# A hybrid attention block: the memory's norm, keys and values move behind the first half's output projection

## The chip, the cores and the metric

The kernel runs on one core of one Trainium2 chip. Its time is the device time of one execution in microseconds (us); the kernel before takes 900.56 us, the median of three runs (899.28 to 900.87). An execution is also recorded by the hardware profiler; the numbers of the trace come from that one. The engines are TensorE (PE: matmuls; PEld: its weight loads), VectorE (DVE), ScalarE (ACT), GpSimd (POOL) and SyncE (SP), which only issues DMAs here. L96 is line 96 of the kernel before.

## The reference

One transformer block on x of 512 rows by 1024, with a memory of 256 rows by 1024. What matters here is its middle part (`_rmsnorm` scales each row by its root mean square and a gain):

```python
# inside the mixer: three branches o_a, o_b, o_c of width 256, gated and summed
g = sigmoid(p['g_merge']).reshape(B, S, 3, D_MODEL)
merged = g[..., 0, :] * (o_a @ w_up[0]) + g[..., 1, :] * (o_b @ w_up[1]) + g[..., 2, :] * (o_c @ w_up[2])
h = x + merged @ w_out                                   # the output projection

def _memory_attention(h, mem, g_q, g_kv, w_q, w_kv, w_o):
    q = (_rmsnorm(h, g_q) @ w_q).reshape(B, S, 4, 64)
    kv = (_rmsnorm(mem, g_kv) @ w_kv).reshape(B, M, 2, 4, 64)
    s = einsum('bshd,bmhd->bhsm', q, kv[:, :, 0]) * 64 ** -0.5
    o = einsum('bhsm,bmhd->bshd', softmax(s), kv[:, :, 1])
    return o.reshape(B, S, 256) @ w_o

h = h + _memory_attention(h, mem, ...)
h = h + _swiglu(_rmsnorm(h, norm_ffn), ...)              # the feed-forward stage (FFN)
```

The keys and values `kv` depend on the memory alone, so they can be computed at any point ahead of the first attention that reads them.

## The kernel before, in words

Every product of fp32 matrices is three matmuls of rounded halves: `mm3` (L91 to L96) issues high by high (L94), high by low (L95) and low by high (L96). An operand's halves are made by `split`: the high one is a cast on ScalarE (L58), the low one a subtraction (L66) on VectorE or GpSimd. A weight tile of 128 by 1024 is fetched by SP (L80) into `raw`, cast into `whi`, subtracted into `wlo`. There are two loaders: `load_split` with three buffers and the subtraction on VectorE, and `load_fill` with two buffers and the subtraction on GpSimd.

The order of the instructions on each engine is not written by hand: a scheduler takes the program and orders it by its own estimates, pools and dependencies. Each engine then runs its list strictly in that order, and an instruction that waits holds up all behind it.

The stretch that the change concerns, in the order of the program before:

1. Gates 2 and `merge_up(2, "c")`: gates of the third branch (`merge_gate`, tanh at L373), then its up projection, whose product is added to the running sum `g_t[0, f]` by GpSimd (L404), for eight feature blocks f.
2. Gates 1, first half: `fill_gate(1, f, S // 2)` for f = 0 to 7, 24 matmuls of 256 columns each into one of two banks `gf`; only the first 256 rows of x.
3. The memory stage (L661 to L683). Two memory chunks of 128 rows are loaded by ScalarE's queue into `h[0]` and `h[1]` (L664), normalised by `norm_t` (L122 to L137: a square with its sum on ScalarE, L127; eight small operations on VectorE, L115 to L120, for the root; the scaling, L129; eight transposes on TensorE, L133; high and low halves into `mem_t`, which is the second half of `mg`), multiplied by `w_mem_kv` in 48 matmuls of 512 columns into the two banks `gm` (L675), copied out; the keys are transposed (L680) into `km` and the values copied into `vm`.
4. `merge_up(1, "b")` for the first half: 48 matmuls of 256 columns, L388 and L401 on VectorE, the halves of the merged rows into the first half of `mg`. Then eight copies (L688, ScalarE) of the second half of the sums into `h[2]` and `h[3]` (`first1`).
5. The loop over halves (L778 on), cp = 0: x into `h[0]`, `h[1]` (L783); the output projection `ob`, 96 matmuls of 512 columns with eight tiles of `w_out` (L790); four adds into h (L794); `memory_pair` (L718): the norm with `gain_q`, the query projection, scores, softmax, the product with the values, the output matrix `w_mem_o`, the adds (L773), and the norm with `gain_f` for the FFN.
6. cp = 1 begins with `merge_rest` (L700): the gates and up projection of the first branch-1 features for the second half. Their matmuls (of 256 columns, into banks `wo`) need nothing of the first half's attention, and the scheduler sets them between the attention's steps, where TensorE would else wait. Then the same as in 5 for the second half, then the FFN.

The names of the tiles: `ut_hi`, `ut_lo` the halves of a normalised and transposed input; `u` the normalised rows; `ss`, `rs` the sum of squares and its root; `prm` the attention's probabilities; `gh` a gate of the second half.

## Time and profile before

| what | value |
|---|---|
| median of 3 runs | 900.56 us (899.28 to 900.87) |
| the profiled execution | 898.28 us |
| its span in the trace | 896.5 us, clock 0.994 of full |
| TensorE busy | 856.3 us (96%), 5012 matmuls and transposes |
| VectorE, ScalarE, GpSimd busy | 507.8, 411.5, 140.7 us |
| the stretch 374.7 to 476.0 us (points 3 to 6) | 101.3 us, TensorE busy 94.9 us |

A row of the trace has the start of an instruction (or of a run of equal ones, then xN), its duration, its engine and line, what it writes and reads, and in brackets how long the engine stood idle before it and which instruction released it. Matmuls overlap, so the time that one costs in a run is the distance between two starts and not its own duration. A window's row gives busy times in a stretch; its length less TensorE's busy time is the idle time there.

### The profile page before, as it was taken

Reading aid. Unit: us, or ns where it says so; the run is one execution under the profiler, and the core shown is the slowest. Engines: PE = TensorE matmul, PEld = TensorE weight load, DVE = VectorE, ACT = ScalarE, POOL = GpSimd, SP = SyncE. Lnnn points to the kernel's source line nnn. Section 1 sums busy time; section 2 is a strip of 40 time slices with the busy share of each in tenths; the row PEclk is TensorE's granted clock in tenths of the full one; section 3 lists DMA queues with packets and bytes.
Section 4 is the critical chain, followed back from the end, with each engine's and each line's share of the span. In section 5 each row is a group of like instructions: output and inputs, shape, how many; then the busy total and the mean of one; then the engine's idle time right before and its main releaser. Section 6 shows DMA issues by size and latency. Waiting matters only on the chain.

```text
span 896.5 us, 13084 instructions
## 1 busy us (share of the span) xinstructions
PE 856.3 (96%) x5012; PEld 731.7 (82%) x5012; DVE 507.8 (57%) x1155; ACT 411.5 (46%) x779; POOL 140.7 (16%) x116
## 2 busy tenths in 40 slices
PE   5999999899989999999989999999999999999995
PEld 5987899787757788978878979988888888888884
DVE  4456378799998305676677758643443334322226
ACT  6487545557774224544654545432322333211123
POOL 4021232302211347430232010000000000000002
PEclk9999999999999999999999999999999999999998
DMA  9340124510210334558446514642333332333312
GB/s 323 85 110 24 43 58 119 141 48 24 70 26 24 95 94 141 187 174 246 125 150 199 165 49 142 187 142 94 97 102 105 97 94 94 118 94 95 99 42 94
DMA packets 93710, 99.00 MB, mean 110 GB/s; under 512 B 4656, under 2 KB 81616, under 8 KB 93648
## 3 DMA queue, kind: packets, MB, share of 16 engines
q1 hardware_dynamic: 91568, 92.75, 34.0%
q10 hardware_dynamic: 2080, 5.42, 1.9%
q8 instruction: 39, 0.64, 0.3%
q14 instruction: 23, 0.19, 0.1%
HBM read 96.06 MB, written 2.10 MB: 109 GB/s over the span
## 4 chain that ended last, share of the span: by engine, by line
PE 85%; DVE 7%; ACT 4%; issue 2%; DMA 1%; POOL 0%; ACTq 0%; DVEq 0%; POOLq 0%
PE wo L95 9%; PE wo L96 9%; PE wo L94 9%; PE gf L94 6%; PE gf L95 6%; PE gf L96 6%; PE ff L94 4%; PE ff L95 4%; PE ff L96 4%; PE gm L94 3%; PE gm L95 3%; PE gm L96 3%; PE y L96 2%; PE y L94 2%; PE y L95 2%; PE av L101 2%
## 5 line engine op out<-in xcount | busy, mean ns | idle before, releaser
L58 ACT CAST whi<-raw 128x1024 fp32r<-128x1024 f32 (+1 forms) x167 | 174.8, 1048 | 292.4 <-PE y L96 78.9
L66 DVE TENSOR_TENSOR wlo<-raw,whi 128x1024 fp32r<-128x1024 f32 (+1 forms) x131 | 164.1, 1255 | 211.2 <-ACT whi L58 210.9
L66 POOL TENSOR_TENSOR wlo<-raw,whi 128x1024 fp32r<-128x1024 f32 x36 | 88.9, 2474 | 312.9 <-ACT whi L58 267.1
L95 PE MATMUL wo<-ut_lo,whi 128*128 128x256 f32 (+1 forms) x320 | 105.2, 329 | 0.0
L96 PE MATMUL wo<-ut_hi,wlo 128*128 128x256 f32 (+1 forms) x320 | 104.6, 327 | 0.0
L94 PE MATMUL wo<-ut_hi,whi 128*128 128x256 f32 (+1 forms) x320 | 104.4, 326 | 0.0
L96 PE MATMUL gf<-ut_hi,wlo 128*128 128x512 f32 (+1 forms) x192 | 69.8, 363 | 0.0
L94 PE MATMUL gf<-ut_hi,whi 128*128 128x512 f32 (+1 forms) x192 | 69.3, 361 | 0.0
L95 PE MATMUL gf<-ut_lo,whi 128*128 128x512 f32 (+1 forms) x192 | 69.3, 361 | 0.0
L94 PE MATMUL ff<-ut_hi,whi 128*128 128x512 f32 (+1 forms) x192 | 67.9, 354 | 0.0
L95 PE MATMUL ff<-ut_lo,whi 128*128 128x512 f32 (+1 forms) x192 | 67.9, 354 | 0.0
L96 PE MATMUL ff<-ut_hi,wlo 128*128 128x512 f32 (+1 forms) x192 | 67.9, 354 | 0.0
L95 PEld LDWEIGHTS wo<-ut_lo,whi 128*128 128x128 f32 x320 | 60.9, 190 | 6.2 <-issue 1.0
L94 PEld LDWEIGHTS wo<-ut_hi,whi 128*128 128x128 f32 x320 | 60.8, 190 | 5.8 <-issue 0.7
L96 PEld LDWEIGHTS wo<-ut_hi,wlo 128*128 128x128 f32 x320 | 60.8, 190 | 5.6 <-issue 0.4
L875 POOL TENSOR_TENSOR ut_hi<-ut_hi,ut_lo 128x512 f32<-128x512 f32 x4 | 5.0, 1276 | 367.0 <-ACT ut_hi L874 367.0
L94 PE MATMUL gm<-whi,ut_hi 128*128 128x256 f32 (+1 forms) x160 | 47.4, 296 | 0.0
L95 PE MATMUL gm<-wlo,ut_hi 128*128 128x256 f32 (+1 forms) x160 | 46.4, 290 | 0.0
L96 PE MATMUL gm<-whi,ut_lo 128*128 128x256 f32 (+1 forms) x160 | 46.3, 289 | 0.0
L96 PEld LDWEIGHTS gf<-ut_hi,wlo 128*128 128x128 f32 x192 | 36.2, 188 | 5.6 <-issue 1.2
L95 PEld LDWEIGHTS gf<-ut_lo,whi 128*128 128x128 f32 x192 | 36.2, 188 | 5.4 <-issue 0.8
L94 PEld LDWEIGHTS gf<-ut_hi,whi 128*128 128x128 f32 x192 | 36.2, 188 | 5.3 <-issue 0.8
(329 smaller groups left out, 2027.7 us busy)
## 6 DMA issues: line engine op xcount, KB each, us to landing
raw<-in_w_ffn_in_dram SPq DMA_DIRECT2D x56, 512.0 KB, 3.6
raw<-in_w_in_dram SPq DMA_DIRECT2D x46, 512.0 KB, 3.9
raw<-in_w_ffn_out_dram SPq DMA_DIRECT2D x22, 512.0 KB, 3.5
raw<-in_w_out_dram SPq DMA_DIRECT2D x16, 512.0 KB, 3.6
raw<-in_w_up_dram SPq DMA_DIRECT2D x8, 512.0 KB, 4.0
xt<-in_x_dram SPq DMA_DIRECT2D x4, 512.0 KB, 9.0
raw<-in_w_mem_kv_dram SPq DMA_DIRECT2D x4, 512.0 KB, 3.8
raw<-in_w_mem_q_dram SPq DMA_DIRECT2D x4, 512.0 KB, 3.8
```

Of the source, the lines that this page charges most:

```text
L58: nc.scalar.copy(dst, src)
L66: (lo_eng or nc.vector).tensor_sub(dst_lo, src, dst_hi.bitcast(F32))
L94: nc.tensor.matmul(dst, lh, rh, start=first, stop=False, skip_group_check=True)
L95: nc.tensor.matmul(dst, lh, rl, start=False, stop=False, skip_group_check=True)
L96: return nc.tensor.matmul(dst, ll, rh, start=False, stop=last, skip_group_check=True).ins
L101: nc.tensor.matmul(dst[64 * x:64 * x + 64], lhs[x], rhs[x], start=first, stop=last, skip_group_check=True)
L875: nc.gpsimd.tensor_mul(yo[:, n], yo[:, n], gain[:, n])
```

## The change

The memory stage goes from its place ahead of `merge_up(1, "b")` into a function `memory_kv()`, called after the first half's output projection is issued and before its adds into h. The raw memory rows then lie in the attention's `prm` tiles and no longer in `h[0]`, `h[1]`; the normalised rows in the pool's `u`; the keys in `qs`; the accumulators are the attention's two banks `mm` in place of `gm`; the transposes use the later pool of banks, which has two. `gain_kv` and `gain_q` take the two gain buffers, and `gain_f` is loaded after `memory_kv()` and handed to `memory_pair`. `mem_t` is still the second half of `mg`.

```diff
--- before.py
+++ after.py
@@ -658,30 +658,6 @@
     mg = (mgp.tile([P, NK, S], F32R, name="mg_hi"), mgp.tile([P, NK, S], F32R, name="mg_lo"))
     half0, half1 = slice(0, S // 2), slice(S // 2, S)
     mem_t = [t[:, :, half1] for t in mg]
-    kv_st = ctx.enter_context(ExitStack())
-    kvp = pool(kv_st, "kvp")
-    for c in range(2):
-        nc.scalar.dma_start(h[c], A["mem"][0, cc(c), :])
-    gain = load_gain(kvp, "norm_mem_kv")
-    for c in range(2):
-        norm_t(kvp, ps, h[c], gain, mem_t, cc(c), u=h[2 + c])
-    kv_acc = [gm_ps.tile([P, 512], F32, name="gm") for c in range(2)]
-    for k2 in range(0, NK, 2):
-        wh, wl = load_split((2, 512), [col_view(A["w_mem_kv"][0], 0, 512)[:, k2:k2 + 2, :]])
-        for kk in range(2):
-            for c in range(2):
-                k = k2 + kk
-                mm3(kv_acc[c], [t[:, k, cc(c)] for t in mem_t], (wh[:, kk, :], wl[:, kk, :]), k == 0, k == NK - 1)
-    for c in range(2):
-        kvt = h[c][:, 0:512]
-        nc.scalar.copy(kvt, kv_acc[c])
-        tp = ps.tile([P, 4, P], F32, name="ps")
-        for i in range(2):
-            nc.tensor.transpose(tp[:, i, :], kvt[:, i * P:(i + 1) * P], ident)
-        nc.vector.tensor_copy(km[:, :, cc(c)], tp[:, 0:2, :])
-        nc.vector.tensor_copy(vm[:, c, :], kvt[:, 256:512])
-    kv_st.close()
-
     merge_up(1, "b", load_split, gm_ps, S // 2)
     first1 = [h[2 + f // 4][:, f % 4 * 256:f % 4 * 256 + 256] for f in range(NK)]
     for f in range(NK):
@@ -712,10 +688,31 @@
             nc.vector.tensor_add(t, t, first1[f])
             split(mg[0][:, f, half1], mg[1][:, f, half1], t, lo_eng=nc.gpsimd)
 
+    gain_kv = load_gain(md, "norm_mem_kv", 2)
     gain_q = load_gain(md, "norm_mem_q", 2)
-    gain_f = load_gain(md, "norm_ffn", 2)
-
-    def memory_pair(cs):
+
+    def memory_kv():
+        for c in range(2):
+            raw = md.tile([P, 4, 256], F32, name="prm", bufs=2).rearrange("p a b -> p (a b)")
+            nc.scalar.dma_start(raw, A["mem"][0, cc(c), :])
+            norm_t(md, ps, raw, gain_kv, mem_t, cc(c))
+        acc = [mm_ps.tile([P, 512], F32, name="mm") for c in range(2)]
+        for k2 in range(0, NK, 2):
+            wh, wl = load_split((2, 512), [col_view(A["w_mem_kv"][0], 0, 512)[:, k2:k2 + 2, :]])
+            for kk in range(2):
+                for c in range(2):
+                    k = k2 + kk
+                    mm3(acc[c], [t[:, k, cc(c)] for t in mem_t], (wh[:, kk, :], wl[:, kk, :]), k == 0, k == NK - 1)
+        for c in range(2):
+            kt = md.tile([P, 256], F32, name="qs")
+            nc.scalar.copy(kt, acc[c][:, 0:256])
+            nc.vector.tensor_copy(vm[:, c, :], acc[c][:, 256:512])
+            tp = ps.tile([P, 4, P], F32, name="ps")
+            for i in range(2):
+                nc.tensor.transpose(tp[:, i, :], kt[:, i * P:(i + 1) * P], ident)
+            nc.vector.tensor_copy(km[:, :, cc(c)], tp[:, 0:2, :])
+
+    def memory_pair(cs, gain_f):
         pr = {}
         for c in cs:
             norm_t(md, ps, h[c], gain_q, uT, cc(c))
@@ -788,11 +785,14 @@
                 for half in range(2):
                     n = slice(half * 512, half * 512 + 512)
                     mm3(ob[c, half], [t[:, k, cc(c)] for t in mg], [t[:, 0, n] for t in w], k == 0, k == NK - 1)
+        if cp == 0:
+            memory_kv()
+            gain_f = load_gain(md, "norm_ffn", 2)
         for c in cs:
             for half in range(2):
                 n = slice(half * 512, half * 512 + 512)
                 nc.vector.tensor_add(h[c][:, n], ob[c, half], h[c][:, n])
-        memory_pair(cs)
+        memory_pair(cs, gain_f)
     dump("h2", h[0])
     mg_st.close()
```

The number of instructions is the same on every engine (1057 rows on VectorE in both lists). On the page of lines, L680 to L683 become L709 to L713, L688 becomes L664, L712 becomes L688, L773 becomes L770; the others named here keep theirs. Since `h[2]`, `h[3]` are no longer used by the memory's norm, the eight copies of `first1` move ahead into gates 1. The scheduler's order moves with it, on VectorE above all, at three places.

VectorE at the up projection of the first half, before (`g_4143`, `g_4176`, ... are the gates f = 0, 1, ...; `wlo_4710` is the first tile of `w_out`):

```order
L388 SCALAR_TENSOR_TENSOR g_4143<-g_4143,gm_4578 128x256
L401 TENSOR_TENSOR g_1119<-g_1119,g_4143 128x256
L388 SCALAR_TENSOR_TENSOR g_4176<-g_4176,gm_4589 128x256
L388 SCALAR_TENSOR_TENSOR g_4209<-g_4209,gm_4600 128x256
L401 TENSOR_TENSOR g_1152<-g_1152,g_4176 128x256
L401 TENSOR_TENSOR g_1185<-g_1185,g_4209 128x256
L388 SCALAR_TENSOR_TENSOR g_4242<-g_4242,gm_4611 128x256
L388 SCALAR_TENSOR_TENSOR g_4275<-g_4275,gm_4628 128x256
L401 TENSOR_TENSOR g_3551<-g_3551,g_4242 128x256
L401 TENSOR_TENSOR g_3584<-g_3584,g_4275 128x256
L388 SCALAR_TENSOR_TENSOR g_4308<-g_4308,gm_4639 128x256
L66 TENSOR_TENSOR wlo_4710<-raw_4707,whi_4709 128x1024
```

and after the change (`wlo_4429`, `wlo_4479` are the tiles of `w_up`, `wlo_4564` and `wlo_4582` the first two of `w_out`):

```order
L66 TENSOR_TENSOR wlo_4429<-raw_4426,whi_4428 128x1024
L66 TENSOR_TENSOR wlo_4479<-raw_4476,whi_4478 128x1024
L388 SCALAR_TENSOR_TENSOR g_4143<-g_4143,gm_4432 128x256
L66 TENSOR_TENSOR wlo_4564<-raw_4561,whi_4563 128x1024
L401 TENSOR_TENSOR g_1119<-g_1119,g_4143 128x256
L388 SCALAR_TENSOR_TENSOR g_4176<-g_4176,gm_4443 128x256
L388 SCALAR_TENSOR_TENSOR g_4209<-g_4209,gm_4454 128x256
L401 TENSOR_TENSOR g_1152<-g_1152,g_4176 128x256
L401 TENSOR_TENSOR g_1185<-g_1185,g_4209 128x256
L388 SCALAR_TENSOR_TENSOR g_4242<-g_4242,gm_4465 128x256
L401 TENSOR_TENSOR g_3551<-g_3551,g_4242 128x256
L388 SCALAR_TENSOR_TENSOR g_4275<-g_4275,gm_4482 128x256
```

The first tile of `w_out` is split ahead of the first gate's sum, where it stood behind that of the sixth.

VectorE at the norm of the second memory chunk, before (`gain_4431` is the memory's gain; the three `wlo` are tiles of `w_mem_kv`):

```order
L129 SCALAR_TENSOR_TENSOR h3_4415<-h1_4413,rs_4461,gain_4431 128x1024
L66 TENSOR_TENSOR wlo_4490<-raw_4487,whi_4489 128x1024
L66 TENSOR_TENSOR wlo_4508<-raw_4505,whi_4507 128x1024
L66 TENSOR_TENSOR wlo_4526<-raw_4523,whi_4525 128x1024
L66 TENSOR_TENSOR mg_lo_4425<-ps_4445,mg_hi_4424 128x4x128
L66 TENSOR_TENSOR mg_lo_4425<-ps_4452,mg_hi_4424 128x4x128
L66 TENSOR_TENSOR mg_lo_4425<-ps_4471,mg_hi_4424 128x4x128
L66 TENSOR_TENSOR mg_lo_4425<-ps_4478,mg_hi_4424 128x4x128
```

and after (`u_4737` is the second normalised chunk, `wlo_4786` and `wlo_4804` are tiles of `w_mem_kv`, `wo_4558` is the output projection's second sum for `h[0]`; the add of the first sum stands two rows further up):

```order
L66 TENSOR_TENSOR wlo_4786<-raw_4783,whi_4785 128x1024
L120 SCALAR_TENSOR_TENSOR rs_4739<-rs_4739 128x1
L794 TENSOR_TENSOR h0_4412<-wo_4558,h0_4412 128x512
L129 SCALAR_TENSOR_TENSOR u_4737<-prm_4734,rs_4739,gain_4551 128x1024
L66 TENSOR_TENSOR mg_lo_4425<-ps_4720,mg_hi_4424 128x4x128
L66 TENSOR_TENSOR mg_lo_4425<-ps_4727,mg_hi_4424 128x4x128
L66 TENSOR_TENSOR wlo_4804<-raw_4801,whi_4803 128x1024
L66 TENSOR_TENSOR mg_lo_4425<-ps_4749,mg_hi_4424 128x4x128
```

The scaling of the second chunk now stands behind the adds into `h[0]`, which need sums of the output projection, and the low halves of both chunks behind that.

VectorE at the norm for the FFN, before (`rs_5115` and `u_5113` belong to chunk 0):

```order
L119 SCALAR_TENSOR_TENSOR rs_5115<-rs_5115 128x1
L120 SCALAR_TENSOR_TENSOR rs_5115<-rs_5115 128x1
L129 SCALAR_TENSOR_TENSOR u_5113<-h0_4412,rs_5115,gain_4699 128x1024
L115 TENSOR_SCALAR rs_5142<-ss_5139 128x1
L117 TENSOR_SCALAR rs_5142<-rs_5142 128x1
L119 SCALAR_TENSOR_TENSOR rs_5142<-rs_5142 128x1
L66 TENSOR_TENSOR wlo_5483<-raw_5480,whi_5482 128x1024
```

and after (`gh_5168` to `gh_5234` are gates of the second half, `wo_5306` and so on their up projections, `rs_5117` and `u_5115` those of chunk 0):

```order
L119 SCALAR_TENSOR_TENSOR rs_5117<-rs_5117 128x1
L388 SCALAR_TENSOR_TENSOR gh_5168<-gh_5168,wo_5306 128x256
L120 SCALAR_TENSOR_TENSOR rs_5117<-rs_5117 128x1
L688 TENSOR_TENSOR gh_5168<-gh_5168,h2_4414 128x256
L119 SCALAR_TENSOR_TENSOR rs_5117<-rs_5117 128x1
L388 SCALAR_TENSOR_TENSOR gh_5201<-gh_5201,wo_5317 128x256
L120 SCALAR_TENSOR_TENSOR rs_5117<-rs_5117 128x1
L115 TENSOR_SCALAR rs_5144<-ss_5141 128x1
L688 TENSOR_TENSOR gh_5201<-gh_5201,h2_4414 128x256
L129 SCALAR_TENSOR_TENSOR u_5115<-h0_4412,rs_5117,gain_4851 128x1024
L117 TENSOR_SCALAR rs_5144<-rs_5144 128x1
L388 SCALAR_TENSOR_TENSOR gh_5234<-gh_5234,wo_5328 128x256
```

Sums of the gates for the second half, which stood in the softmax before, stand between the steps of the root; behind them, past the halves of chunk 0, comes the split of the next gate's weights.

## Rows read from the trace of the kernel before

**Rows 1.** Which engine sets the end: the page's busy time, share and count of each engine.

```profile
PE 856.3 (96%) x5012; PEld 731.7 (82%) x5012; DVE 507.8 (57%) x1155; ACT 411.5 (46%) x779; POOL 140.7 (16%) x116
```

**Rows 2.** The span in stages: busy time and count by engine, clock, DMA share, GB/s.

```profile
374.70:389.00 14.30, 13.59 (x67) 10.70 (x66) 7.57 (x9) 9.66 (x19) 0.81 (x1) 1.00 0.53 171
389.00:396.40 7.40, 7.06 (x54) 6.42 (x54) 6.73 (x16) 4.04 (x8) 3.86 (x5) 1.00 0.66 215
396.40:420.15 23.75, 22.34 (x97) 17.60 (x96) 15.68 (x17) 9.64 (x12) 5.03 (x4) 1.00 0.77 236
420.15:435.80 15.65, 15.38 (x131) 15.20 (x130) 11.84 (x28) 9.34 (x15) 1.44 (x1) 1.00 0.53 146
435.80:461.00 25.20, 23.81 (x164) 19.44 (x163) 17.38 (x32) 15.77 (x36) 8.86 (x7) 1.00 0.47 148
461.00:476.00 15.00, 12.76 (x106) 12.35 (x105) 14.26 (x28) 8.73 (x15) 3.28 (x2) 1.00 0.47 144
```

**Rows 3.** TensorE where the memory stage stands now: start, length, operation, idle before and releaser.

```profile
374.73 1.47 PE L133 MATMUL ps<-cst,h 128*128 128x128 f32 x12
...
376.67 0.50 PE L94 MATMUL gm<-whi,mg_hi 128*128 128x512 f32 x1 [0.47 <-ACT mg_hi L58]
...
377.65 0.51 PE L94 MATMUL gm<-whi,mg_hi 128*128 128x512 f32 x1 [0.25 <-ACT mg_hi L58]
...
378.35 0.48 PE L96 MATMUL gm<-whi,mg_lo 128*128 128x512 f32 x1
```

**Rows 4.** TensorE in the output projection of the first half, and its end.

```profile
400.81 0.50 PE L95 MATMUL wo<-wlo,mg_hi 128*128 128x512 f32 x1 [0.65 <-DVE wlo L66]
...
409.37 0.50 PE L95 MATMUL wo<-wlo,mg_hi 128*128 128x512 f32 x1 [0.77 <-DVE wlo L66]
...
419.93 0.39 PE L96 MATMUL wo<-whi,mg_lo 128*128 128x512 f32 x1
420.15 0.28 PE L94 MATMUL wo<-ut_hi,whi 128*128 128x256 f32 x1
420.26 0.28 PE L95 MATMUL wo<-ut_lo,whi 128*128 128x256 f32 x1
```

**Rows 5.** ScalarE: the gates' tanh, the load of a gain, and a weight cast that waits for DMA.

```profile
354.89 0.39 ACT L373 ACTIVATE g<-gf 128x256 f32<-128x256 f32 x1 [0.85 <-PE gf L96]
...
399.66 0.34 ACTq L140 DMA_DIRECT2D gain<-in_norm_mem_q_dram  x1
...
407.00 1.05 ACT L58 CAST whi<-raw 128x1024 fp32r<-128x1024 f32 x1 [5.35 <-DMA raw<-in_w_out_dram]
```

**Rows 6.** GpSimd: adds of the third branch, and a weight split beside the norm.

```profile
346.07 10.77 POOL L404 TENSOR_TENSOR g<-g 128x512 f32<-128x512 f32 x7
...
462.79 2.39 POOL L66 TENSOR_TENSOR wlo<-raw,whi 128x1024 fp32r<-128x1024 f32 x1 [0.90 <-POOL wlo L66]
```

**Rows 7.** VectorE: prices of an add into h and of a weight split.

```profile
418.31 0.69 DVE L794 TENSOR_TENSOR h<-wo,h 128x512 f32<-128x512 f32 x1 [0.71 <-PE wo L96]
418.92 1.22 DVE L66 TENSOR_TENSOR wlo<-raw,whi 128x1024 fp32r<-128x1024 f32 x1
```

**Rows 8.** TensorE at the transposes for the query projection.

```profile
426.45 1.06 PE L133 MATMUL ps<-cst,u 128*128 128x128 f32 x8 [0.27 <-DVE rs L120]
```

**Rows 9.** VectorE in the norm for the feed-forward stage of the first half.

```profile
462.90 2.30 DVE L120 SCALAR_TENSOR_TENSOR rs<-rs 128x1 f32<-128x1 f32 x1
...
465.68 1.28 DVE L129 SCALAR_TENSOR_TENSOR u<-h,rs,gain 128x1024 f32<-128x1024 f32 x1
...
468.52 1.28 DVE L66 TENSOR_TENSOR ut_lo<-ps,ut_hi 128x512 fp32r<-128x512 f32 x2
...
475.80 0.41 DVE L712 TENSOR_TENSOR gh<-gh,h 128x256 f32<-128x256 f32 x1
```

**Rows 10.** TensorE in the same norm: the last gate matmul, the transposes that wait.

```profile
464.50 0.28 PE L94 MATMUL wo<-ut_hi,whi 128*128 128x256 f32 x1
467.02 1.09 PE L133 MATMUL ps<-cst,u 128*128 128x128 f32 x8 [2.24 <-DVE u L129]
```

## The prediction

> **What bounds the kernel now.** I read the page's busy times first: TensorE is busy for 856.3 of 896.5 us, no other engine for more than 57% [rows 1]. The same matmuls are issued before and after the change, so it can only move TensorE's idle time. Next I read the windows by stage: from 374.7 to 476.0 us they show the granted clock at 1.00, which is the 2.4 GHz level, in every stage, and TensorE busy for 13.59 of 14.30, 7.06 of 7.40, 22.34 of 23.75, 15.38 of 15.65, 23.81 of 25.20 and 12.76 of 15.00 us, 94.9 of 101.3 in all [rows 2]. Then the timelines, for what ends each idle time. In the output projection it is twice the split of a weight tile on VectorE (0.65 and 0.77 us) [rows 4]; at the memory stage the cast of the normalised rows on ScalarE (0.47 and 0.25) [rows 3]; ahead of the FFN norm's transposes the scaled rows on VectorE (2.24) [rows 10]. Outside this stretch the lists of instructions are the same but for the end of gates 1, so I follow TensorE's list through the stretch, stage by stage, and count what each stage's wait becomes. The unit prices: a matmul of 512 columns 0.2267 us (419.93 to 420.15 is one of them), one of 256 columns 0.12 (420.15 to 420.26) [rows 4], a transpose 0.105 to 0.12 (twelve in 1.47) [rows 3], a split of a weight tile on VectorE 1.22, an add into h 0.69 [rows 7], a scaling of 128x1024 1.28, two splits of 512 columns 1.28 together, a gate's add 0.41 [rows 9], a cast on ScalarE 1.05 [rows 5].
>
> **The change part by part.**
>
> *Gates 1, the copies of first1.* Nothing is added, but eight copies on ScalarE move ahead, seven of them into a place where they wait for GpSimd's adds of the third branch, which end at 346.07 + 10.77 = 356.84 [rows 6]. Behind the last copy (some 0.35, half of an add's 0.69) stand one weight cast (1.05) and the tanh of the first gate (0.39, at 354.89 now [rows 5]), which frees one of two banks. It would be free at 356.84 + 0.4 + 1.05 + 0.3 = 358.6. The third gate wants it at 374.73 less six gates of 24 x 0.12 = 2.88, that is 357.5 [rows 3]. So 1.1 us are lost if GpSimd's adds take what they take now, none if they end 1.1 us sooner because the memory's norm no longer runs on VectorE beside them. I take +0.4, ends 0 and +1.1.
>
> *The up projection of the first half.* It takes 7.40 us now [rows 2] for 48 matmuls of 0.12, which is 5.8, with a matmul of the next stage, the keys' transposes and about 1.2 us of waits among them. VectorE gets a weight split ahead of the first gate's add, so the fourth gate's matmuls wait for a bank once; the waits stay about 1.1. I take -0.1, ends -0.6 and +0.4.
>
> *The output projection.* It takes 23.75 us [rows 2] for 95 matmuls, 95 x 0.2267 = 21.54: 2.2 us are lost, 1.42 of them in the two waits for splits [rows 4]. The cause is the ring of three weight buffers: it held the memory's weights until that stage ended, so the tiles of w_out were fetched late; one of them kept ScalarE waiting for 5.35 us [rows 5]. After the change these tiles come first, and VectorE splits the first of them ahead of the first gate's add. Some 0.3 us stay. I take -1.9; the ends are -2.1 (nothing left) and 0 (two gains, as the one issued at 399.66 [rows 5], and two memory chunks of the same size share the DMA engines, which are busy for 0.77 of this stage already [rows 2]).
>
> *The memory stage and the query projection.* What they lose now: 374.73 to 378.35 is 3.62 us for 16 transposes and three matmuls, which would take 2.4 [rows 3]; with 0.2 at the keys' transposes that is 1.4. The query projection's transposes wait for 0.27 [rows 8], with a like wait at the second chunk 0.5; together 1.9. After the change the scaling of the second chunk waits on VectorE behind the two adds into h[0], which need the output projection's sums. The first of these adds starts 1.84 us before that projection's end now (418.31 against 420.15) [rows 4, 7]; call the end T. Then: first add to T - 1.15, a small operation and a weight split to T + 0.3, the second add to T + 1.1, the scaling to T + 2.4, two splits of the first chunk to T + 3.7, a weight split to T + 4.9, the low half of the second chunk's first four blocks at T + 5.5. TensorE needs that half after 16 transposes and five matmuls, 1.7 + 1.1 = 2.8. So it loses 2.7, say 2.6 with a little overlap. Behind the stage the copies of keys and values stand on VectorE among weight splits of 1.22 each, and there are two banks for transposes: the transposes of h wait until the second chunk's keys are copied. Between 0.5 (covered, as now) and 2.4 (two splits uncovered); I take 1.5, the gate matmuls that the order puts there covering the rest. Together 4.1 against 1.9: +2.2, ends -0.5 and +4.
>
> *The attention.* 25.20 us, TensorE busy for 23.81 [rows 2]. The order has 86 gate matmuls as cover now and 69 after; 17 go to later places. A weight split (1.22) stands between two row maxima and three weight casts (1.05 each) ahead of exponentials. I take half of one of them, +0.6, ends -0.5 and +1.5.
>
> *The norm for the FFN.* The attention's product ends at about 461.0; 30 gate matmuls cover it to 464.6, the transposes start at 467.02: 2.4 us lost [rows 10], 2.5 with the second chunk. One small operation of the root took 2.30 us there while GpSimd split a weight tile (462.79, 2.39) [rows 6, 9]. After the change four gate adds of 0.41 [rows 9] stand among the steps of the root: the scaled rows come not 6.0 but 7.6 us after the product's end. The cover is 40 matmuls, 4.8 us: 2.8 lost. Then the weight split of the next gate stands behind that scaling, four more adds (1.4), two splits of the transposed rows (1.28) and five small operations (1.0), with its own 1.22 some 4.9 in all, while TensorE has the transposes (1.0) and 15 matmuls (1.8): 2.0 more lost. So 4.8 against 2.5: +2.3. The ends: -0.5 (a quarter of the wait now gone, no other wait) and +4.
>
> The Trainium skill, page "SBUF — State Buffer", section "Who interferes with whom", says that a VectorE operation with two inputs in SBUF and a GpSimd operation that reads SBUF exclude each other, whoever starts first, while one with an input in PSUM doesn't take part. The trace agrees: the small operation at 462.90 took 2.30 us beside GpSimd's 2.39 [rows 6, 9]. By that rule one of the second half's adds, or a small operation, blocks in the same place after the change, and the sum stays; if that row were a mishap of one execution, the norm would lose about 2.1 us less after the change, and the sum would be +1.4.
>
> The sum: 0.4 - 0.1 - 1.9 + 2.2 + 0.6 + 2.3 = +3.5 us. Against the profiled execution, 898.28, that is 901.8. That execution is 2.28 us below the median of the runs, 900.56; runs of the changed kernel are compared with that median, so the forecast is 900.56 + 3.5 = 904.1, rounded to 904.0.
>
> **The rivals.**
>
> *The weights ahead decide (faster).* The output projection gives -2.1 and the new neighbours on VectorE cost little, because the engine is busy for only half to two thirds of the stages around and has caught up where I count a wait: the memory stage and query projection at 0, the attention at -0.3, the norm at -0.5. That is -2.9: 897.7. For it: VectorE's 15.68 of 23.75 us in the projection [rows 2]. Against it: two adds that can't start before the projection's sums are done, whatever VectorE did before.
>
> *Gains and waits cancel (no change).* The waits at the memory stage and the norm come at half their size, 1.1 each, the attention at +0.3: 0.4 - 0.1 - 1.9 + 1.1 + 0.3 + 1.1 = +0.9, so 901.5. For it: my order of events puts every instruction as late as its list allows. Against it: both places had idle time of that kind before, with less in the queue.
>
> *The memory rows come late (slower still).* The two chunks and two gains are fetched while the tiles of w_out are; a tile kept ScalarE waiting for 5.35 us in that stage [rows 5]. If the square of a chunk waits so on ScalarE, the casts of the next tiles wait behind it, the projection's gain is lost (+1.9) and the memory stage starts 1.5 later: 904.0 + 3.4 = 907.4. Against it: the chunks are asked for a whole projection of 23.75 us ahead.
>
> That the change moves nothing is ruled out by the order shown.
>
> **How the numbers follow.** Forecast 0.47, slower still 0.13, no change 0.23, faster 0.17. A measurement of this kernel tells 0.2%, that is 1.8 us, from no change. So faster by more than that 0.17, within it 0.23, slower 0.60. The range of the likeliest case alone is 902.4 to 906; the range that should hold the time reaches to the rivals on both sides, 898.0 to 907.4.
>
> **What would show it.** Right: in the profile of the changed kernel TensorE runs through the output projection in about 21.8 us; then waits of together over 2 us for the low halves or scaled rows of the memory, released by VectorE; waits of together over 4 us from the attention's end to the next output projection, one of them for a weight split. Wrong: if the memory stage starts without a wait of over 1 us, the fourth term falls; if the transposes of the FFN norm wait for less than 2 us and no weight split is waited for, the sixth; if the projection still takes over 23 us, the third. The forecast as a whole is wrong if the stretch from the last matmul of gates 1 to the second output projection is not longer than 101.3 us.

## The result and the profile after

The kernel after takes 908.29 us, the median of four runs (905.60 to 908.67), against 899.92 us (898.47 to 900.87) for the kernel before in four runs beside it: the medians lie 8.4 us apart, and the ratio is 1.0088 (95% interval 1.0063 to 1.0113), so the kernel after is slower. The forecast was 904.0, slower by 3.5, in a range of 898.0 to 907.4. The direction was right; the size came out 2.4 times as large and the time 0.9 us above the range.

The profiled execution took 908.67 us, the longest of the four; its span is 906.6 against 896.5. So the two traces differ by 10.1 us where the medians differ by 8.4: what follows accounts for this pair of executions. The page of the kernel after, busy time by engine and the granted clock in 40 slices (to hold against [rows 1]):

```profile
PE 862.9 (95%) x5012; PEld 736.9 (81%) x5012; DVE 500.5 (55%) x1155; ACT 411.2 (45%) x779; POOL 137.1 (15%) x116
PEclk9999999999999998999999999999999999999998
```

The same 5012 instructions keep TensorE busy for 6.6 us longer. Idle time is not in that figure, so the first reading was the windows by stage, with the clock. Columns as in [rows 2]: busy time and count of PE, PEld, DVE, ACT, POOL, then clock, DMA share and GB/s; the kernel after:

```profile
341.30:349.00 7.70, 6.42 (x29) 5.07 (x27) 3.54 (x4) 3.60 (x6) 6.13 (x4) 1.00 0.40 114
349.00:356.40 7.40, 6.08 (x16) 4.97 (x17) 3.10 (x5) 1.82 (x5) 3.78 (x3) 0.55 0.22 71
356.40:378.70 22.30, 22.30 (x189) 22.30 (x188) 4.99 (x5) 9.99 (x17) 11.07 (x5) 1.00 0.54 163
378.70:409.40 30.70, 28.75 (x146) 23.67 (x145) 21.76 (x40) 15.24 (x23) 9.43 (x9) 1.00 0.67 223
409.40:426.90 17.50, 14.82 (x66) 11.85 (x65) 15.44 (x35) 8.81 (x13) 0.00 (x0) 0.90 0.58 157
426.90:437.60 10.70, 10.70 (x89) 10.23 (x89) 6.07 (x10) 5.09 (x8) 1.40 (x1) 1.00 0.49 143
437.60:461.30 23.70, 22.69 (x148) 18.12 (x147) 13.04 (x23) 13.33 (x31) 4.78 (x3) 1.00 0.39 112
461.30:485.75 24.45, 21.69 (x168) 21.28 (x167) 20.99 (x40) 13.61 (x24) 7.30 (x6) 0.93 0.51 167
```

The stages are the third branch's up projection with gates 1 (the first three rows), the first half's up projection with the output projection, the memory stage, the query projection, the attention, and the norm for the FFN with the gate matmuls set there. The clock was 1.00 in every stage of [rows 2]; here three rows show 0.55, 0.90 and 0.93. The second row has 16 matmuls in 7.4 us: an idle time, and then matmuls at the 1.2 GHz level. The last row is long mostly because 62 more gate matmuls stand in it.

TensorE's timeline of the kernel after (start, length, instruction, idle time before it and releaser):

```profile
347.44 0.28 PE L94 MATMUL gf<-ut_hi,whi 128*128 128x256 f32 x1
350.31 0.80 PE L94 MATMUL gm<-o_hi,whi 128*128 128x512 f32 x1 [2.59 <-DVE g L388]
...
352.19 0.63 PE L95 MATMUL gm<-o_lo,whi 128*128 128x512 f32 x1
352.61 0.63 PE L96 MATMUL gm<-o_hi,wlo 128*128 128x512 f32 x1
...
381.97 0.39 PE L94 MATMUL gm<-o_hi,whi 128*128 128x256 f32 x1 [0.82 <-DVE g L388]
...
387.43 0.39 PE L94 MATMUL gm<-o_hi,whi 128*128 128x256 f32 x1 [0.68 <-DVE g L388]
...
409.43 1.03 PE L133 MATMUL ps<-cst,u 128*128 128x128 f32 x8
411.92 0.50 PE L94 MATMUL mm<-whi,mg_hi 128*128 128x512 f32 x1 [1.46 <-ACT mg_hi L58]
...
413.88 0.66 PE L133 MATMUL ps<-cst,u 128*128 128x128 f32 x4 [1.22 <-DVE mg_lo L66]
...
468.40 1.28 PE L133 MATMUL ps<-cst,u 128*128 128x128 f32 x8 [2.24 <-DVE rs L117]
...
473.80 0.39 PE L94 MATMUL wo<-ut_hi,whi 128*128 128x256 f32 x1 [0.52 <-ACT whi L58]
```

Matmuls of 512 columns start 0.42 us apart at 352, against 0.2267 in [rows 4]. The longest wait among these, 2.59 us at 350.31, is in the third branch's up projection, and before the change no such wait is there. The chain that ended last in this stretch, in order of time (start, length, what):

```profile
344.85 1.26 POOL g L404
...
346.13 0.41 ACT h L664
346.54 0.96 ACT whi L58
...
347.52 2.14 DVE wlo L66
349.66 0.61 DVE g L388
...
350.31 0.80 PE gm L94
```

Read upward from TensorE: the matmul waits for a bank `gm`, which VectorE's product L388 frees; that stands in VectorE's list behind a weight split, which waits for a cast; the cast stands in ScalarE's list behind one of the moved copies of `first1` (L664), and that copy waits for GpSimd's add. "The change" had put these copies into gates 1; the first of them stands at 346.13, in the up projection ahead of them. The split takes 2.14 us instead of 1.22 [rows 7].

The Trainium skill, page "SBUF — State Buffer", section "Who interferes with whom", says that a VectorE operation with two inputs in SBUF and a GpSimd operation that reads SBUF shut each other out. The split, which starts at 347.52, has two such inputs, and a run of GpSimd's adds lasts until 348.58; its 2.14 us agrees. Before the change a split stood beside such adds as well (347.06, 1.39 us) and made no wait.

The accounting, from TensorE's starts in the two timelines. Gate matmuls that only fill gaps are taken out of the last three stages at 0.12 us each (65, 86 and 89 before, 20, 69 and 151 after: 240 in both):

| stage | before | after | change | forecast |
|---|---|---|---|---|
| up to the third branch's up projection | 342.58 | 341.31 | -1.27 | 0 |
| third branch's up projection, gates 1 | 32.03 | 37.28 | +5.25 | +0.4 |
| first half's up projection, output projection | 31.01 | 30.61 | -0.40 | -2.0 |
| memory stage, query projection | 22.14 | 25.79 | +3.65 | +2.2 |
| attention | 14.92 | 15.36 | +0.44 | +0.6 |
| norm for the FFN | 4.32 | 6.37 | +2.05 | +2.3 |
| the rest | 420.47 | 420.80 | +0.33 | 0 |

They add up to +10.1, the difference of the spans. The first row is not the change: over all the profiles below this start lies between 341.1 and 343.8, by where the clock fell in the first 340 us (341.1 to 341.3 in the five with one fall at about 172 us, the kernel after among them; the kernel before has its fall at 269).

What the clock takes is best read from the same list at full clock. Behind the first wait that list takes 34.5 us for the stage (`a_ufirst` and `a_dveq`; `b_early` and `a_dummy` below agree), so 2.8 of the 37.28 are clock. In the norm it takes 5.70 us (`a_hold_mem` below, with the same instructions in the same order on every engine and the same wait of 2.24 us), so 0.7 of the 6.37 are clock. The window would give 24.45 x 0.07 = 1.7 there, but at half clock TensorE is busy for 1.05 us longer and idle for 0.4 less, so part of the slower work falls on time that is idle at full clock. For the memory stage no run has the same list at full clock: the window gives 17.50 x 0.10 = 1.7 as an upper end, a near list (`a_hold` against `a_hold_kvwarm` below) 1.0. Together the clock takes an estimated 4.5 to 5.2 of the 10.1 us.

### The profile page after: what moved, and what is told of

Same layout as the page of the kernel before. It is cut to its first block, busy times and chain, and to the rows that moved or that the text cites. A ratio compares the mean times of both kernels' runs of the same rounds, so it can differ in the third digit from the quotient of the medians.

```text
span 906.6 us, 13086 instructions
## 1 busy us (share of the span) xinstructions
PE 862.9 (95%) x5012; PEld 736.9 (81%) x5012; DVE 500.5 (55%) x1155; ACT 411.2 (45%) x779; POOL 137.1 (15%) x116
## 4 chain that ended last, share of the span: by engine, by line
PE 83%; DVE 7%; ACT 4%; DMA 2%; issue 2%; POOL 1%; ACTq 0%; SPq 0%; DVEq 0%; POOLq 0%
PE wo L95 8%; PE wo L94 8%; PE wo L96 8%; PE gf L95 6%; PE gf L94 5%; PE gf L96 5%; PE ff L96 4%; PE ff L94 4%; PE ff L95 4%; PE gm L94 3%; PE gm L95 3%; PE gm L96 2%; PE y L96 2%; PE y L95 2%; PE y L94 2%; PE av L101 2%
```

## The experiments

Three theories: (A) the copies of `first1`, through the chain above, make the first wait; (B) the rest is the memory stage's waits, where VectorE holds the scaling behind the adds into h, as the prediction had it; (C) each such wait brings the clock to half, and that is as dear as the waits themselves. The rival to A is that the moved memory stage is dear in itself. Every run is compared with the kernel before on the same chip (898.7 to 899.4 us).

### a_hold and b_early: the copies alone, taken out and put in

`a_hold` is the kernel after with the copies put behind the last tanh in ScalarE's order; `b_early` is the kernel before with the memory's norm writing into tiles of its own pool, so that the scheduler may issue the copies early while the memory stage stays.

```diff
 a_hold
-            nc.scalar.activation(g, bank, AF.Tanh, scale=0.5)
+            last_tanh[0] = nc.scalar.activation(g, bank, AF.Tanh, scale=0.5).ins
...
-    for f in range(NK):
-        nc.scalar.copy(first1[f], g_t[0, f][:, half1])
+    with tc.issue_after(last_tanh[0]):
+        [nc.scalar.copy(first1[f], g_t[0, f][:, half1]) for f in range(NK)]
 b_early
-        norm_t(kvp, ps, h[c], gain, mem_t, cc(c), u=h[2 + c])
+        norm_t(kvp, ps, h[c], gain, mem_t, cc(c))
```

> The changed kernel with the eight copies of first1 held behind the last tanh of gates 1. Theory (the copies on ScalarE wait for GpSimd's adds, hold a weight cast, VectorE's split and adds wait for that, TensorE idles 2.6 us and its clock then stands at half for some 6 us): the stretch from the third branch's up projection to the end of gates 1 goes from 37.4 back to about 32.1 us, the clock stays at full there, and the time is about 908.3 - 5.3 = 903. Rival (the loss sits in the moved memory stage, the stall of 2.6 us is a matter of one execution): 908, and the stretch stays above 36 us or the loss appears later.

> The kernel before with one thing changed: the memory's normalised rows go into tiles of their own instead of h[2] and h[3], so that the copies of first1 move ahead into gates 1 as they do after the change. The memory stage stays where it was. Theory: the stall of 2.6 us and the half clock come alone, 899.9 + 5 = about 905. Rival (the memory stage's new place is the cause): 900, no stall over 1 us in the third branch's up projection.

Measured: `a_hold` 905.87 us (6 runs), ratio 1.0070 (1.0053 to 1.0087); `b_early` 903.40 (9 runs, 900.55 to 906.39), ratio 1.0049 (1.0033 to 1.0064). The same stage as a window, in `a_hold`:

```profile
343.80:376.10 32.30, 32.18 (x233) 30.29 (x232) 11.45 (x12) 13.00 (x19) 22.00 (x12) 1.00 0.52 157
```

TensorE is busy for 32.18 of 32.30 us at full clock; by starts the stage takes 32.04 us, as before the change (32.03). In `b_early` the wait appears without any other part of the change (the last row is the norm for the FFN):

```profile
350.17 0.50 PE L94 MATMUL gm<-o_hi,whi 128*128 128x512 f32 x1 [2.60 <-DVE g L388]
350.50 0.39 PE L95 MATMUL gm<-o_lo,whi 128*128 128x512 f32 x1
350.73 0.39 PE L96 MATMUL gm<-o_hi,wlo 128*128 128x512 f32 x1
...
467.65 1.09 PE L133 MATMUL ps<-cst,u 128*128 128x128 f32 x8 [2.26 <-DVE rs L115]
```

So the copies make the first wait: theory A holds from both sides. But behind an equal wait (2.60 against 2.59) the matmuls start 0.23 apart here (350.50 to 350.73): the clock stayed at 1.00. The windows of `b_early`, this place and the norm for the FFN:

```profile
349.00:356.40 7.40, 6.24 (x41) 5.73 (x42) 5.34 (x7) 3.26 (x7) 5.09 (x4) 1.00 0.47 144
467.50:478.00 10.50, 10.35 (x76) 10.35 (x77) 8.85 (x19) 4.81 (x8) 0.00 (x0) 0.84 0.49 148
```

and the kernel before at that norm:

```profile
467.00:477.50 10.50, 10.47 (x82) 9.97 (x83) 10.27 (x23) 6.21 (x11) 0.00 (x0) 1.00 0.57 185
```

The norm's wait is 2.26 us in `b_early` and 2.24 before [rows 10]; one is followed by half clock, the other is not. Theory C as put, that each such wait brings the clock down, falls. A wait may be followed by it, and then the same list costs between 0.7 us (the norm after the change) and 2.8 us (the first wait) more; `b_early`'s norm takes 16.34 us against 15.00 before. The profile of `b_early` (900.70 us) is one of the shortest of its nine runs, whose median is 903.40; the runs at 0.987 to 0.990 of full clock are those above 903. In the runs `a_hold` gains less than the 5.2 us its stage gives: its ratio lies 0.0018 (1.6 us) under that of the kernel after, inside both intervals, so the runs alone do not tell the two apart. In its profile the stage starts at 343.84, 2.5 us later than in the kernel after, and the memory stage with the query projection is 0.9 us longer.

### a_dummy: the wait filled, not removed

The kernel after with eleven matmuls of no use (512 columns, into a spare bank) where the first wait is.

```diff
                 nc.gpsimd.tensor_add(first, first, g)
+                dk = gf_ps.tile([P, 512], F32, name="gf") if f == 4 else None
+                [nc.tensor.matmul(dk, w[0][:, 0, 0:P], oT[name][0][:, 0, :], start=True, stop=True, skip_group_check=True) for _ in range(11 if f == 4 else 0)]
```

> The changed kernel with 11 extra matmuls of 512 columns (2.5 us) on TensorE ahead of the matmuls that wait in the third branch's up projection; they write a bank that nothing reads. The waiting chain through ScalarE, VectorE and GpSimd is unchanged. If the half clock after the stall is caused by TensorE's idleness, the matmuls behind the wait start at the same time but at full clock: about 908.3 - 2.7 = 905.6. If the slow matmuls have another cause (operands or banks still busy): 908 to 911, with the clock at half there all the same.

Measured: 906.49 us (6 runs), ratio 1.0076 (1.0061 to 1.0091). TensorE's timeline and two windows from there on:

```profile
347.11 2.65 PE L404 MATMUL gf<-o_hi,whi 128*128 128x512 f32 x11
349.60 0.39 PE L94 MATMUL gm<-o_hi,whi 128*128 128x512 f32 x1
349.82 0.39 PE L95 MATMUL gm<-o_lo,whi 128*128 128x512 f32 x1
```

```profile
349.00:353.00 4.00, 3.75 (x17) 2.79 (x16) 2.91 (x3) 0.68 (x2) 2.23 (x3) 1.00 0.27 66
353.00:357.00 4.00, 4.00 (x31) 3.74 (x30) 3.01 (x3) 2.21 (x5) 3.50 (x3) 1.00 0.19 71
```

The stage takes 34.60 us against 37.28: the time of the wait is still lost, the clock's part is not. The matmuls behind the wait start 0.22 us apart, as at 2.4 GHz. That prices the clock. That the added matmuls kept it up is not shown by one profile, since it also held without them in `b_early`, `a_ufirst` and `a_dveq`. The runs hint at it: their mean clock is 0.990 to 0.992 here, 0.987 to 0.990 in the kernel after and 0.987 to 0.991 in `a_ufirst`. The ratio is 0.0012 (1.1 us) under that of the kernel after, which the intervals alone do not tell apart.

The Trainium skill, page "TensorE: Matmul & The Clock Gate", section "What's actually happening", says that the clock follows how busy TensorE has lately been. That fits the filled wait; the trace adds that waits of one length are not always followed by the same level.

### a_ufirst: the scaling ahead of the adds into h

The kernel after with VectorE's four adds into h (L794) put behind the second chunk's scaling: the mechanism that the prediction named for its fourth term.

```diff
-        nc.vector.scalar_tensor_tensor(u, src, y, gain, op0=ALU.mult, op1=ALU.mult)
+        scaled[0] = nc.vector.scalar_tensor_tensor(u, src, y, gain, op0=ALU.mult, op1=ALU.mult).ins
...
-        for c in cs:
-            for half in range(2):
+        with tc.issue_after(scaled[0]):
+            for c, half in ob:
```

> The changed kernel with the adds of the output projection into h held behind the scaling of the second memory chunk on VectorE. Theory of the prediction (the second chunk stands behind two adds that wait for the projection): the waits at the start of the memory stage, 1.46 and 1.22 us, shrink to under 1.5 together, the clock may stay at full there (another 1.3), time 905.5 to 907. Rival (the stage waits for ScalarE's casts of the normalised rows, which have a late weight cast before them): the first wait stays at 1.4, only the second goes, 907 to 908.5.

Measured: 907.60 us (5 runs), ratio 1.0095 (1.0080 to 1.0110): no gain. Four lines of its VectorE timeline, and two of TensorE's:

```profile
409.10 1.28 DVE L129 SCALAR_TENSOR_TENSOR u<-prm,rs,gain 128x1024 f32<-128x1024 f32 x1
410.29 0.68 DVE L794 TENSOR_TENSOR h<-wo,h 128x512 f32<-128x512 f32 x1
410.89 1.22 DVE L66 TENSOR_TENSOR wlo<-raw,whi 128x1024 fp32r<-128x1024 f32 x1
412.02 1.28 DVE L66 TENSOR_TENSOR mg_lo<-ps,mg_hi 128x512 fp32r<-128x512 f32 x2
```

```profile
409.79 0.50 PE L94 MATMUL mm<-whi,mg_hi 128*128 128x512 f32 x1 [1.22 <-ACT mg_hi L58]
...
412.76 1.12 PE L133 MATMUL ps<-cst,u 128*128 128x128 f32 x4 [2.25 <-DVE mg_lo L66]
```

The scaling starts 1.80 us behind the projection's last matmul (407.30) in place of 2.75 (411.95 against 409.20), and the waits are 1.22 + 2.25 in place of 1.46 + 1.22. Theory B falls in the form that the prediction gave it: with the scaling ahead of the adds the waits do not shrink. VectorE's list still sets the second wait, by another instruction: the second chunk's transposes wait for one of the two banks, which comes free when the first chunk's low half (`mg_lo`) has been made from it. In this kernel an add and a weight split stand ahead of that, and the transposes start at 412.76, as its first half is done. No kernel was run with the low halves ahead of adds and splits. What makes the first wait is in ScalarE's timeline of the kernel after:

```profile
410.34 1.04 ACT L58 CAST whi<-raw 128x1024 fp32r<-128x1024 f32 x1 [1.24 <-DMA raw<-in_w_mem_kv_dram]
411.29 1.07 ACT L58 CAST mg_hi<-ps 128x512 fp32r<-128x512 f32 x2
```

The high halves of the first chunk's normalised rows are cast at 411.29, though their transposes start at 409.43: they stand behind the cast of a tile of `w_mem_kv` that waits for its DMA. This cause is read from the rows; no kernel changed that order.

### a_hold_mem and a_hold_kvwarm: the memory's rows early, the memory stage's waits filled

`a_hold_mem` is `a_hold` with the memory's rows in two tiles of their own, loaded before gates 1. `a_hold_kvwarm` is `a_hold` with twenty matmuls of 256 columns, of no use, at the start of the memory stage (`dums` issues them; `trs` lists the transposes of `norm_t`, so they come behind those of the first chunk).

```diff
 a_hold_mem
+    memr = [mkv.tile([P, D], F32, name=f"memr{c}") for c in range(2)]
+    [nc.scalar.dma_start(memr[c], A["mem"][0, cc(c), :]) for c in range(2)]
-            raw = md.tile([P, 4, 256], F32, name="prm", bufs=2).rearrange("p a b -> p (a b)")
-            nc.scalar.dma_start(raw, A["mem"][0, cc(c), :])
+            raw = memr[c]
 a_hold_kvwarm
         acc = [mm_ps.tile([P, 512], F32, name="mm") for c in range(2)]
+        with tc.issue_after(trs[-9]): dums(acc[0], 20)
```

> The kernel a_hold with one thing more: the two memory chunks have tiles of their own and are loaded before gates 1, so nothing on ScalarE's queue delays them. Theory A (the memory stage starts late because its rows are asked for in the middle of ScalarE's list and wait there behind casts and with the w_out tiles for the DMA engines): the squares come before the middle of the output projection, the waits at the stage's start (2.31 and 1.21 us in a_hold) go under 1 us together, the clock stays at full there (another 1.6), time 905.9 - 4 = 902. Theory B (the adds into h on VectorE are what the stage waits for): the first wait shrinks little, 905 or more.

> The kernel a_hold with 20 extra matmuls of 256 columns (2.4 us) on TensorE at the start of the memory stage, where it waits for the memory's halves; they write a bank that nothing has used yet. If the half clock behind this wait comes from TensorE's idleness, the clock stays at full to the end of the stage and the time falls by up to 1.6 us, to about 904.5, although TensorE has more to do. If not: the clock falls all the same, 906 to 908.

Measured: `a_hold_mem` 903.12 us (9 runs, 899.32 to 904.32), ratio 1.0036 (1.0022 to 1.0050); `a_hold_kvwarm` 903.63 (6 runs), ratio 1.0048 (1.0032 to 1.0064). The first lies clear of `a_hold`'s ratio (1.0053 to 1.0087), the second overlaps it at the edge. TensorE in `a_hold_mem`, whose squares run at 387.50 and 392.85 (after the change at 402.67 and 404.66, the second row load issued only at 397.83, when ScalarE was done waiting 4.16 us for a tile of `w_out`):

```profile
405.14 0.50 PE L94 MATMUL mm<-whi,mg_hi 128*128 128x512 f32 x1 [1.48 <-ACT mg_hi L58]
...
406.52 0.66 PE L133 MATMUL ps<-cst,u 128*128 128x128 f32 x4 [0.64 <-DVE mg_lo L66]
```

In `a_hold` these waits are 2.31 and 1.21; early rows take 1.4 us off them, and 1.48 stay. The first of them has another cause on ScalarE in `a_hold`:

```profile
408.38 0.34 ACTq L140 DMA_DIRECT2D gain<-in_norm_ffn_dram  x1
408.76 1.07 ACT L58 CAST mg_hi<-ps 128x512 fp32r<-128x512 f32 x2 [3.19 <-DVE u L129]
```

The load of `gain_f` stands ahead of the cast and needs the buffer of the memory's gain, which the second chunk's scaling frees; that ran at 407.07, behind an add into h. So there the scaling behind an add does reach TensorE, through ScalarE's list. With early rows the scaling runs at 399.26.

The granted clock is 1.00 in all stages of the profile of `a_hold_mem`, which is that of its fastest run; the other eight runs show 0.988 to 0.992. `a_hold_kvwarm` and, below it, `a_hold`, over the memory stage:

```profile
409.00:412.00 3.00, 1.79 (x13) 1.63 (x14) 3.00 (x5) 2.59 (x5) 0.00 (x0) 1.00 0.88 255
412.00:418.00 6.00, 6.00 (x28) 4.92 (x27) 5.84 (x22) 3.46 (x5) 0.00 (x0) 1.00 0.35 93
```

```profile
409.00:412.00 3.00, 1.40 (x7) 0.96 (x7) 3.00 (x6) 2.83 (x5) 0.00 (x0) 0.92 0.77 234
412.00:418.00 6.00, 6.00 (x24) 4.96 (x23) 5.66 (x21) 2.86 (x5) 0.00 (x0) 0.76 0.52 146
```

A wait of 1.99 us is left behind nineteen of the added matmuls, and the clock stays. From the output projection's last matmul to the query projection's last the stage takes 28.07 us against 29.07; the nineteen stand in time that was idle without them. So the memory stage too pays for the clock, 1.0 us by this pair, beside the 1.4 for the late rows. That the matmuls kept the clock up is likely and not shown by one profile: the mean clock of the runs is 0.988 to 0.994 here, five of six at 0.991 or more, and 0.986 to 0.990 in `a_hold`.

### b_dveo, a_best, b_dveq, a_hold_mem_q, a_dveq, b_dveqo: the norm for the FFN

In both kernels a small operation of the root takes over 2 us while GpSimd splits a weight tile (2.30 in [rows 9], 2.07 after). `b_dveo` lets VectorE split `w_mem_o` instead; `b_dveq` lets it split the second half's `w_mem_q`. Both start from the kernel before. `b_dveqo` has both edits. `a_dveq` is the kernel after with the second edit, `a_hold_mem_q` is `a_hold_mem` with it; `a_best` joins `a_hold_mem`, `a_ufirst` and the first edit.

```diff
 b_dveo
-    w = load_fill((2, 512), [col_view(A["w_mem_o"][0], half * 512, 512)])
+    w = load_fill((2, 512), [col_view(A["w_mem_o"][0], half * 512, 512)], lo_eng=nc.vector)
 b_dveq
-    w = load_fill((4, 256), [col_view(A["w_mem_q"][0], 0, 256)[:, 4 * kh:4 * kh + 4, :]])
+    w = load_fill((4, 256), [col_view(A["w_mem_q"][0], 0, 256)[:, 4 * kh:4 * kh + 4, :]], lo_eng=nc.vector if cs[0] else nc.gpsimd)
```

> The kernel before with one thing changed: the low halves of w_mem_o are made by VectorE instead of GpSimd. By the rule that a VectorE operation with two SBUF inputs and a GpSimd operation that reads SBUF exclude each other, the small operation of 2.30 us in the FFN norm of the first half falls to 0.2, the transposes wait for 0.3 us instead of 2.24: 898.7 - 2 = 896.7. If the norm is late for another reason, or the four more splits of 1.22 us on VectorE delay the attention: 898.5 to 900.

> The changed kernel with all four: the copies of first1 held, the memory chunks loaded early, the adds into h behind the scaling of the second chunk, the low halves of w_mem_o by VectorE. If the changed order loses by these four waits and the clock behind them alone, it comes to the time of the kernel before or under it: 897 to 900 (the output projection's gain of 1 to 2 us is then left over). If the order itself costs more: 902 or above.

> The kernel before with one thing changed: the low halves of the second half's w_mem_q, which GpSimd makes beside the first half's FFN norm, are made by VectorE. If GpSimd's split is what holds the small operation of the root for 2.3 us (each reads SBUF through a port that they share), that operation falls to 0.2 us and the wait of the transposes from 2.24 to 1.2 or less (one of the two splits, 1.22, now stands ahead of the root on VectorE); the clock then has no idle time behind which to fall; time 899.3 - 1 to - 2.2 = 897.1 to 898.3 and fewer runs above 900. If the operation is long for another reason: it stays at 2.3 and the time rises by 1.2 to 900.5.

> The kernel a_hold_mem with the same change as b_dveq. If the wait of 2.24 us in the FFN norm and the half clock behind it are what is left of the loss, 903.1 - 2 to - 3.5 = 899.6 to 901 and the spread of the runs narrows; if the loss sits in the memory stage's order, 902.5 or more.

> The changed kernel with the change of b_dveq alone. The waits at the third branch and the memory stage stay with their clock falls; the FFN norm's wait and its clock fall (2.24 and 1.7 us) go or halve: 908.3 - 2 to - 4 = 904.3 to 906.3. If the norm waits for the second half's gate adds on VectorE instead: 907 to 909.

> The kernel before with both changes of b_dveo and b_dveq: VectorE makes the low halves of w_mem_o and of the second half's w_mem_q. If their gains add (-1.2 and -4.2 against before): 899.4 - 5.4 = 894.0. If the four splits together crowd VectorE ahead of the FFN norm: 895 to 897.

Measured:

| kernel | us (runs) | ratio to before |
|---|---|---|
| `b_dveo` | 897.91 (12) | 0.9989 (0.9978 to 0.9999) |
| `a_best` | 901.17 (12) | 1.0022 (1.0009 to 1.0034) |
| `b_dveq` | 895.20 (6) | 0.9954 (0.9939 to 0.9970) |
| `a_hold_mem_q` | 900.80 (12) | 1.0017 (1.0004 to 1.0030) |
| `a_dveq` | 906.33 (6) | 1.0073 (1.0055 to 1.0092) |
| `b_dveqo` | 895.17 (5) | 0.9957 (0.9943 to 0.9971) |

`b_dveo` moved the wrong split. Its VectorE timeline still has

```profile
463.48 2.33 DVE L120 SCALAR_TENSOR_TENSOR rs<-rs 128x1 f32<-128x1 f32 x1
```

beside a GpSimd split at 463.39. That split is of the second half's `w_mem_q`, fetched ahead, as the next kernel shows. With that one moved, VectorE and TensorE in `b_dveq`:

```profile
463.25 0.16 DVE L120 SCALAR_TENSOR_TENSOR rs<-rs 128x1 f32<-128x1 f32 x1
...
463.90 1.28 DVE L129 SCALAR_TENSOR_TENSOR u<-h,rs,gain 128x1024 f32<-128x1024 f32 x1
```

```profile
465.24 1.09 PE L133 MATMUL ps<-cst,u 128*128 128x128 f32 x8 [0.23 <-DVE u L129]
```

The operation takes 0.16 us, TensorE's wait of 2.24 [rows 10] is 0.23, and the stretch from the attention's end to the second output projection takes 13.23 us in place of 15.23. That kernel beats both: 895.20 against 899.42 for the one before beside it. The profile gives 2.0 of those 4.2 us at this place; that most of the rest is clock that no longer falls is argued from the runs: all six show a mean clock of 0.994, the seventeen of the kernel before 0.989 to 0.994 with a median of 0.992, and 0.002 of 897 us is 1.8 us. `b_dveqo` adds nothing to it. In the kernel after the edit is worth little (906.33): there the transposes still wait 0.93 us, a further wait of 1.11 for a weight split comes behind, and the clock falls. `a_best` came between its two forecasts: its order has a new wait of 2.52 us in the norm, with half clock behind it. The profile of `a_hold_mem_q`, its fastest run, shows what is left at full clock by the table's stages: -1.8 in the up and output projection, +1.9 in the memory stage and query projection, +0.7 in the attention, nothing in the norm, +0.7 behind it. None of the kernels run with the memory stage moved came under the kernel before.

## Why the prediction was right in direction and wrong in size

**Term 1, gates 1 and the copies (+0.4, measured +5.25): the step that failed.** The prediction named the place (copies waiting for GpSimd's adds), but followed only what stands behind the *last* copy on ScalarE, the tanh that frees a bank `gf`. Behind an *earlier* copy stands a weight cast, behind its split on VectorE the products that free the banks `gm`, and TensorE came to a stop in the third branch's up projection, a stage that the sum did not contain. The wait was 2.59 us, and 2.8 of clock came with it. `a_hold` and `b_early` show that it is the copies. In the sum this term alone takes the time out of the range (904.0 + 4.85); the stages behind it grew by 5.7 us with the clock and an estimated 3.3 to 4.0 without, where 3.1 was forecast.

**The clock, taken as 1.00 throughout.** The prediction took every price from full-clock rows, since [rows 2] had no other. That was the second failed step: it cost an estimated 4.5 to 5.2 of the 10.1 us. Without these the difference would be 4.9 to 5.6, of which the start of the stretch, 1.27 sooner by chance, already hides some.

**Terms 2 and 3, up and output projection (-2.0, measured -0.40).** The output projection gained 1.44 of the 1.9, 22.3 us by the starts, so the third term stands by its own mark of 23. The up projection lost 1.04 where -0.1 was put: its gates wait for banks twice (0.82 and 0.68), not once.

**Term 4, memory stage and query projection (+2.2, measured +3.65).** Size near, 1.95 to 2.65 without the clock; mechanism wrong in its first half. The waits of 1.46 and 1.22 were of the forecast order (2.6), but the first is released by ScalarE, and with the scaling ahead of the adds they did not shrink (`a_ufirst`). The second does go by VectorE's list, through a bank for the transposes. Behind them, where 1.5 was put for the query projection's transposes, the trace has no wait of over 0.2 us. The rival of late memory rows had a part in it: early rows take 1.4 us off the waits (`a_hold_mem`). Its other half, a lost gain in the projection, did not come.

**Terms 5 and 6, attention and norm (+0.6 and +2.3, measured +0.44 and +2.05).** The attention's size was right; no run tested its reason. In the norm, the gate sums among the steps of the root and the blocked small operation are there, but the wait is 2.24 (2.8 was forecast), and in place of one for a weight split (2.0 was forecast) there is one of 0.52 for a weight's cast on ScalarE. 0.7 of the measured 2.05 is clock, so the waits gave 1.4 of the 2.3: part of the agreement is luck. The split wait does appear, 1.11 us, once the first wait is shortened (`a_dveq`).

**The other rivals.** The weights ahead did not decide, and gains and waits did not cancel. (The first rival's -2.9 leaves out the first two terms, +0.3; with them it is 898.0, the lower end of the range.)

What stays open: which execution pays for a wait with the clock, and how often, and so why `a_hold`, which takes the first wait away, gains so little in the runs. The runs of one kernel spread with their mean clock (the kernel after: 905.60 at 0.990, 908.67 at 0.987); behind the first wait the clock fell in one profile and held in three (`b_early`, `a_ufirst`, `a_dveq`, the stage at 34.5 us); what decides it was not found.

## What to carry to other kernels

When a change frees a buffer, look at what else may now be issued earlier, and follow each instruction that moves ahead through the in-order lists of every engine behind it, to the next bank that TensorE wants, not only the last of them. Where TensorE is busy for 95%, price a new wait like these (2.2 to 2.6 us) twice: by its length, and by its length with a stretch at half clock behind it. And price that stretch from the same list at full clock, since part of it can fall on time that would be idle anyway. A tiny operation that takes 2 us beside another engine's long one can be worth more than a large reordering: here one argument that moved the two splits of a weight to VectorE gave 4.2 us.

## What the runs showed of the hardware that was not expected

A wait of 2.6 us on TensorE was followed by six us at 1.2 GHz in the kernel after (350.3 to 356.4) and by none in `b_early`; the norm's wait of 2.24 to 2.26 us by half clock in `b_early` and by none before. With eleven or twenty matmuls of no use in such a wait the clock stayed up in the profile and the stage was shorter (37.28 to 34.60, 29.07 to 28.07 us). And one small operation on VectorE took 14 times its usual time beside a GpSimd split (2.30 against 0.16 us), and TensorE's wait shrank by 2.01 us when that split was gone (2.24 to 0.23).
